# Prompt keys turned by VectorE, the norm factor inside the softmax, and one table load for logarithm and exponential in a hybrid decoder step

## The chip, the cores and the metric

The kernel runs on one core of one Trainium2 chip. The metric is the device time of one execution in microseconds (us). Beside it stands the profiled execution, whose trace gives every instruction of the five engines: TensorE (PE, with its weight loads as PEld), VectorE (DVE), ScalarE (ACT), GpSimd (POOL) and SyncE (SP). POOL and SP issue the DMAs.

## The reference

One layer of a hybrid decoder is computed for 256 prompt tokens and 8 sample sequences of 4 tokens, 288 columns in all, in fp32:

```
xn = rmsnorm(x, norm_mix)
z, xbc, dt, q, k, v, r, g_lr, gate_a, gate_b = split(xn @ w_in)
u = ssd_scan(silu(causal_conv(xbc)), dt, ...) * silu(z)        # Mamba-2 branch, 4 groups
branch_a = rmsnorm_per_group(u, ssd_norm) @ w_ssd_out
glog = log_sigmoid(g_lr @ w_gla_gate + b_gla_gate) / 16
o = gla_scan(q, k, v, glog, ...)                               # gated linear attention, 4 heads
branch_b = (rmsnorm_per_head(o, gla_norm) * silu(r)) @ w_gla_out
h = x + (sigmoid(gate_a) * branch_a + sigmoid(gate_b) * branch_b) @ w_mix_out
# cross-attention, 4 heads of 512, 256 memory tokens; prompt keys and values are
# rmsnorm(mem_prompt) @ w_ck and @ w_cv (also outputs), those of the samples come from a cache
q = rmsnorm(h, norm_cross) @ w_cq
h = h + (softmax(q @ mem_k.T / sqrt(512)) @ mem_v) @ w_co
up = causal_conv(rmsnorm(h, norm_ffn) @ w_up)                  # ConvFFN, 5632 wide
y = rmsnorm(h + (silu(gt) * a) @ w_down, norm_final)
```

The outputs are y, the new states of both branches and of the convolutions, and the prompt's memory keys and values.

## The kernel before, in words

**Projections.** Activations are held transposed: features on the 128 partitions, 288 tokens along the free dimension. `proj` and `proj_w` (L133 to L169) multiply them by a weight matrix, 256 output columns at a time. SyncE loads a weight piece of two row blocks into a tile `raw` (128x512, 256 KB, 6 buffers). `wsplit` (L100) makes two tiles of it, 5 buffers each: ScalarE casts the high part `whi` (L103), VectorE subtracts to get the low part `wlo` (L105). TensorE multiplies three times, high by high and high by low (L148, L149) and low by high (L153). One such step is 12 matmuls of 288 columns; a full projection of 2048 rows and 256 columns has 8 steps and fills two PSUM tiles `acc`, which the consumer function (`cons`) empties. The `acc` tiles have two tags with two buffers each, used in turn, so that a projection takes up the tiles of the one before the last.

**Order of work.** The program stands in a block with a timeline-simulating scheduler (L44). It decides each engine's order of instructions at build time, except where `keep_in_program_order` or a manual schedule holds them. Each engine then executes its list strictly in that order.

**Stages.** First come the memory keys and values of the prompt, written to the outputs o_pmk and o_pmv. Then come eight units, four of the Mamba-2 branch and four of the linear attention (GLA). The scan of each unit is woven with the projections of the next and with the output projection of the one before (`weave`, L180). A unit ends in `finish` (L981): squares are summed over partitions with a matmul by ones (L989), `rstd_from` (L230) takes Ln (L232) and Exp (L233) on ScalarE, and the result is scaled and split into `un`. The group of the Mamba-2 branch also has `gate_early` (L1271), which takes tanh of a quarter of gate_a. A GLA scan begins with `decays` (L1034), with Abs, Exp, Ln (L1045 to L1047) and later Exp (L1053).

Next comes `gate_b` (L1416): the eight projections of the second gate. Its consumer takes tanh of a PSUM tile into `th` (3 buffers, L1418), does two VectorE operations with the branches (L1419, L1420) and splits the result into `mx`. Between these, GpSimd loads four pieces of the merged first branch (`load_mix`, tiles `mar`, 2 buffers), four sample key tiles `kc` of head 0 (`key_load`, 1 MB each), and the residual `hx`. A load that must not come too early is tied to a consumer by a one-column copy on GpSimd from `th` into the tile that is to be loaded. VectorE turns the sample keys in 32x32 blocks (`turn32`, L1386).

`w_mix_out` follows and leaves sums of squares in `sqa`. In cross-attention the next head's query projection (`q_proj`, L1533) is woven with `attend` (L1559) of the present head. The row sum of squares becomes a factor for each of the 288 columns by a matmul with ones (`rstd_of`, L1449), Ln and Exp. The evictions of the queries multiply by that factor (`qs` L1545, `qsm` L1547). `rows_load` brings a head's prompt keys and values in rows; `transpose_half` (L1521) turns the keys with 8 TensorE transposes of 128x128 in a head (L1527) into PSUM, from where they are split into `kTh` and `kTl`. All tiles of keys and values share a ring of five 1 MB buffers (`ring`, L1355). Then come w_co, the ConvFFN (more than a third of the time) and the last norm.

Of the kernel before, what the change touches and what calls it, by code (L numbers as in the profile page):

```python
# [8 lines left out]
F32 = mybir.dt.float32  # L9
F32R = mybir.dt.float32r  # L10
I32 = mybir.dt.int32
ACT = mybir.ActivationFunctionType
# [30 lines left out]
def hybrid_step(ctx: ExitStack, tc: tile.TileContext, I: dict, O: list):  # L43
# [31 lines left out]
    ones = const.tile([P, P], F32, name="ones")  # L75
    V.memset(ones, 1.0)
    epsc = const.tile([P, 3], F32, name="epsc")
    V.memset(epsc[:, 0:1], EPS)
    V.memset(epsc[:, 1:2], 4.0 * EPS)
    fold4 = const.tile([P, NS], F32, name="fold4")  # L80
# [146 lines left out]
    def two(u, n):  # L227
        return lambda k: (u[:, k, :], u[:, n + k, :])

    def rstd_from(pl, ssq, n, four=False):  # L230
        r = pl.tile([P, T], F32, tag="rstd", bufs=1, name="rstd")
        S.activation(r, ssq, ACT.Ln, scale=1.0 / n, bias=epsc[:, 1:2] if four else epsc[:, 0:1])  # L232
        S.activation(r, r, ACT.Exp, scale=-0.5)  # L233
        return r
# [39 lines left out]
    ga_d = dram.tile([P, KT // 2, T], F32, name="ga_d")  # L274
    x_d = dram.tile([D, T], F32, name="x_d")
    h_d = dram.tile([P, KT, T], F32, name="h_d")

    X = halves(bigr, "xn")
    with pool("p0") as p0:
# [736 lines left out]
    def gla_proj(h, out):  # L1016
# [17 lines left out]
        def decays():  # L1034
# [231 lines left out]
            yield from proj(I["w_in"], o + 256 * j2, 256, X, KT, cons)  # L1266

    gq = []
    GH = KT // 4

    def gate_early(t, a):  # L1271

        if t % 2 == 0:
            gq.append(e2("gq"))
        S.activation(gq[-1][:, t % 2, :], a, ACT.Tanh, scale=0.5)
        if t % 2:
            G.dma_start(out=ga_d[:, t - 1:t + 1, :], in_=gq[-1])

# [89 lines left out]
    def rows_load(hd):  # L1368

        t = ktiles[hd, "p"] = ring("kvp")  # L1370
        for w, src in ((0, o_pmk), (1, o_pmv)):
            tc.keep_in_program_order(G.dma_start(out=t[:, 1024 * w:1024 * w + 1024].rearrange("p (m d) -> p m d", m=2),
                                                 in_=src[0, :, hd, :].rearrange("(m p) d -> p m d", p=P)))

    def values(b, hd):
        return I["cache_mem_v"][b, :, hd, :].rearrange("(p h) d -> p h d", h=2)
# [35 lines left out]
        hx.append(m)  # L1412

    load_mix(0)

    def gate_b(t, a):  # L1416
        th = pc.tile([P, T], F32, tag="th", bufs=3, name="th")
        S.activation(th, a, ACT.Tanh, scale=0.5)  # L1418
        V.scalar_tensor_tensor(th, th, 1.0, mb[:, t, :], ALU.add, ALU.mult)  # L1419
        V.tensor_tensor(th, th, mas[t // 4][:, t % 4, :], ALU.add)  # L1420
# [27 lines left out]

    def rstd_of():  # L1449
        ssq = mm_tile()  # L1450
        tc.keep_in_program_order(MM(ssq[:, 0:T], ones, rst.pop(), start=True, stop=True))
        return rstd_from(pb, ssq[:, 0:T], D)

    rst = []
# [33 lines left out]
    for z in (*xqm, pms):  # L1488
        G.memset(z, 0.0)

    def softmax(src, n, out):
        mx = px.tile([P, 1], F32, tag="mx", bufs=3, name="mx")
        V.tensor_reduce(mx[0:n], src, axis=AX.X, op=ALU.max)
        V.tensor_scalar(mx[0:n], mx[0:n], -SC, None, ALU.mult)
        sm = px.tile([P, 1], F32, tag="sm", bufs=3, name="sm")
        S.activation(out, src, ACT.Exp, scale=SC, bias=mx[0:n], accum_out=sm[0:n])
        V.reciprocal(sm[0:n], sm[0:n])
        S.activation(out, out, ACT.Identity, scale=sm[0:n])

    def swapped(t, name):  # L1500

# [5 lines left out]
    def softmax_halves(src, out):  # L1507

        mx = px.tile([P, 1], F32, tag="mx", bufs=3, name="mx")
        V.tensor_reduce(mx, src, axis=AX.X, op=ALU.max)  # L1510
        mo = swapped(mx, "mo")
        V.tensor_scalar(mx, mx, mo, -SC, ALU.max, ALU.mult)
        sm = px.tile([P, 1], F32, tag="sm", bufs=3, name="sm")
        S.activation(out.rearrange("p (m t) -> p t m", t=4), src.rearrange("p (t m) -> p t m", t=4), ACT.Exp, scale=SC, bias=mx,
                     accum_out=sm)
        so = swapped(sm, "so")
        V.tensor_tensor(sm, sm, so, ALU.add)
        V.reciprocal(sm, sm)
        S.activation(out, out, ACT.Identity, scale=sm)

    def transpose_half(kv, d2):  # L1521

        a = mm_tile()
        for d in range(2):
            for m in range(2):
                dd = 2 * d2 + d
                TR(a[:, d * 256 + m * P:d * 256 + (m + 1) * P], kv[:, m, dd * P:(dd + 1) * P], ident)  # L1527
        return a.rearrange("p (d m) -> p d m", m=256)

    qps = []  # L1530
    rc = []

    def q_proj(hd):  # L1533

        if not rc:
            late.append(lambda: mids.append([6, lambda: rc.append(rstd_of())]))
        qp = []
        qps.append(qp)
        for j2 in range(2):
            def cons(j, a, j2=j2):  # L1540
                if j == 0:
                    qp.append((q2("qh"), q2("ql")))
                d = 2 * j2 + j
                qs = px.tile([P, SEQ], F32, tag="qs", bufs=1, name="qs")
# [14 lines left out]
    def attend(hd):  # L1559
# [21 lines left out]
                key_load(hd + 1, c)  # L1581
        yield
        yield
        kvp = ktiles[hd, "p"].rearrange("p (w m d) -> p w m d", w=2, m=2)
        kh, kl = r4("kTh"), r4("kTl")
        for d2 in range(2):
            a = transpose_half(kvp[:, 0], d2)
            split(kh[:, 2 * d2:2 * d2 + 2, :], kl[:, 2 * d2:2 * d2 + 2, :], a)
        yield
        yield  # L1590
        prs = []
        for l in range(2):
# [11 lines left out]
            softmax(a[:, 0:256], P, pp)  # L1604
            prs.append(pp)
            yield
        yield
        vh, vl = v2("vph"), v2("vpl")
        split(vh, vl, kvp[:, 1])
        if more:  # L1610
            key_load(hd + 1, 2)
        yield
# [343 lines left out]
```

## Time and profile before

| | us |
|---|---|
| median of 3 runs (lowest, highest) | 2484.65 (2481.55, 2485.2) |
| the profiled execution | 2484.34 |
| span of its trace, first to last instruction | 2482.6 |
| TensorE busy | 2466.9 |
| VectorE busy | 1769.0 |
| ScalarE busy | 1343.4 |
| GpSimd busy | 436.1 |

The granted TensorE clock was 0.998 over the span. A row of a timeline reads: start in us, duration in us, engine, source line, operation, output tile <- input tiles, shape, count; in brackets the idle time of the engine before it and what ended it. A row of the grouped view reads: busy us, mean ns of one. "The chain of waits" is the chain of work that ended last, each piece with what released it.

### The profile page before, as it was taken

To read this page: it belongs to the slowest core of one execution; us is meant where nothing else is said; L and a number is where in the kernel's file an instruction comes from. 1 tells how busy PE (TensorE), PEld (TensorE's weight loads), DVE (VectorE), ACT (ScalarE), POOL (GpSimd) and SP (SyncE) were. 2 spreads that over 40 slices of the span, in tenths; PEclk is the share of its full clock that TensorE was granted. 3 is DMA by queue.
4 is the path that set the end of the run, shared out by engine and by line. 5 is a ranking of instruction groups with operands and counts; after the bars stand their busy time and mean duration, and the time that the engine had idled before them with its cause. 6 is when DMAs were issued, how large, how long until landed. Compare 5 with 4: busy or idle time off the path is not lost.

```text
span 2482.6 us, 52081 instructions
## 1 busy us (share of the span) xinstructions
PE 2466.9 (99%) x18766; PEld 2387.6 (96%) x18766; DVE 1769.0 (71%) x3794; ACT 1343.4 (54%) x2733; POOL 436.1 (18%) x792
## 2 busy tenths in 40 slices
PE   9999999999999999999999999999999999999998
PEld 8889999999999999999999998999999999999998
DVE  6756778896877666777666577667777676676766
ACT  6656647646464655544555545555555454554545
POOL 3102135143111010110111122402111001020012
PEclk9999999999999999999999999999999999999999
DMA  8877697787769686877777698656555555555555
GB/s 257 250 225 201 167 270 216 205 249 223 230 210 295 200 261 184 249 252 221 234 234 252 204 342 306 195 164 172 170 172 172 172 170 173 170 172 168 170 173 170
DMA packets 457075, 528.66 MB, mean 213 GB/s; under 512 B 40252, under 2 KB 403612, under 8 KB 456784
## 3 DMA queue, kind: packets, MB, share of 16 engines
q1 hardware_dynamic: 420272, 422.39, 56.6%
q0 software_dynamic: 36512, 102.93, 13.0%
q8 instruction: 147, 2.41, 0.4%
q14 instruction: 112, 0.92, 0.1%
q10 hardware_dynamic: 32, 0.01, 0.0%
HBM read 476.41 MB, written 48.76 MB: 212 GB/s over the span
## 4 chain that ended last, share of the span: by engine, by line
PE 95%; DMA 2%; issue 1%; DVE 1%; ACT 0%; POOL 0%; DVEq 0%; POOLq 0%; ACTq 0%
PE acc L149 27%; PE acc L148 27%; PE acc L153 27%; PE acc L328 2%; PE acc L329 2%; PE acc L332 2%; DMA kc<-in_cache_mem_k_dram 1%; PE mm L1239 1%; PE la L1230 1%; PE la L1576 1%; PE mm L1194 0%; DMA raw<-in_w_ssd_out_dram 0%; DMA vc<-in_cache_mem_v_dram 0%; PE la L903 0%; PE mm L924 0%
## 5 line engine op out<-in xcount | busy, mean ns | idle before, releaser
L103 ACT CAST whi<-raw 128x512 fp32r<-128x512 f32 x1464 | 899.7, 618 | 965.2 <-PE acc L149 781.7
L105 DVE TENSOR_TENSOR wlo<-raw,whi 128x512 fp32r<-128x512 f32 x1464 | 996.6, 686 | 549.2 <-ACT whi L103 536.4
L149 PE MATMUL acc<-xn,whi 128*128 128x288 f32 (+1 forms) x1936 | 541.5, 296 | 0.0
L148 PE MATMUL acc<-xn,whi 128*128 128x288 f32 (+1 forms) x1936 | 539.8, 294 | 0.3 <-ACT whi L103 0.3
L153 PE MATMUL acc<-xn,wlo 128*128 128x288 f32 (+1 forms) x1936 | 408.2, 292 | 0.0
L149 PE MATMUL acc<-hf,whi 128*128 128x288 f32 x1408 | 393.1, 296 | 0.0
L148 PE MATMUL acc<-hf,whi 128*128 128x288 f32 x1408 | 388.7, 292 | 0.0
L148 PEld LDWEIGHTS acc<-xn,whi 128*128 128x128 f32 (+1 forms) x1936 | 363.3, 188 | 5.1 <-issue 2.3
L149 PEld LDWEIGHTS acc<-xn,whi 128*128 128x128 f32 (+1 forms) x1936 | 363.7, 188 | 3.6 <-issue 0.4
L153 PEld LDWEIGHTS acc<-xn,wlo 128*128 128x128 f32 (+1 forms) x1936 | 310.4, 188 | 0.9 <-issue 0.4
L153 PE MATMUL acc<-hf,wlo 128*128 128x288 f32 x1408 | 294.5, 290 | 0.0
L149 PEld LDWEIGHTS acc<-hf,whi 128*128 128x128 f32 x1408 | 264.5, 188 | 0.0
L148 PEld LDWEIGHTS acc<-hf,whi 128*128 128x128 f32 x1408 | 264.0, 188 | 0.0
L153 PEld LDWEIGHTS acc<-hf,wlo 128*128 128x128 f32 x1408 | 226.3, 188 | 0.1
L149 PE MATMUL acc<-pr,whi 128*128 128x288 f32 x704 | 196.6, 295 | 0.0
L148 PE MATMUL acc<-pr,whi 128*128 128x288 f32 x704 | 194.8, 293 | 0.0
L1749 POOL COPY fsp<-fst 128x16 f32<-128x16 f32 x88 | 37.3, 427 | 650.7 <-DVE av L1761 431.4
L153 PE MATMUL acc<-pr,wlo 128*128 128x288 f32 x704 | 147.3, 290 | 0.0
L148 PE MATMUL acc<-un,whi 128*128 128x288 f32 x512 | 143.0, 295 | 2.5 <-ACT vT L1020 1.5
L149 PE MATMUL acc<-un,whi 128*128 128x288 f32 x512 | 142.9, 295 | 0.0
L149 PEld LDWEIGHTS acc<-pr,whi 128*128 128x128 f32 x704 | 132.3, 188 | 0.0
L148 PEld LDWEIGHTS acc<-pr,whi 128*128 128x128 f32 x704 | 132.0, 188 | 0.0
(551 smaller groups left out, 4301.9 us busy)
## 6 DMA issues: line engine op xcount, KB each, us to landing
raw<-in_w_in_dram SPq DMA_DIRECT2D x480, 256.0 KB
raw<-in_w_up_dram SPq DMA_DIRECT2D x352, 256.0 KB
raw<-in_w_down_dram SPq DMA_DIRECT2D x176, 256.0 KB
raw<-in_w_ck_dram SPq DMA_DIRECT2D x64, 256.0 KB
raw<-in_w_cv_dram SPq DMA_DIRECT2D x64, 256.0 KB
raw<-in_w_ssd_out_dram SPq DMA_DIRECT2D x64, 256.0 KB
sin<-in_state_gla_dram POOLq DMA_DIRECT2D x32, 512.0 KB, 6.2
out_dram<-sin SPq DMA_DIRECT2D x32, 512.0 KB
```

What stands on the lines that cost most here:

```text
L103: S.copy(hi, raw)
L105: V.tensor_tensor(lo, raw, hi, ALU.subtract)
L148: MM(a, hi[:, k, cs], xh, start=(k0 + s0 + k == 0), stop=False)
L149: MM(a, hi[:, k, cs], xl, start=False, stop=False)
L153: MM(a, lo[:, k, cs], xh, start=False, stop=(k0 + s0 + k == nk - 1))
L328: MM(accs[m], mn_hi[:, kk, ms_], hi[:, 0, :], start=(kk == 0), stop=False)
L329: MM(accs[m], mn_lo[:, kk, ms_], hi[:, 0, :], start=False, stop=False)
L332: MM(accs[m], mn_hi[:, kk, ms_], lo[:, 0, :], start=False, stop=(kk == KT - 1))
L1230: MM(osa[NS * j:NS * j + NS, :], qdm[:, k, b, :], sins[b][:, k, :], start=False, stop=(q == 1 and k == 0))
L1239: MM(a, kb[:, k * P:(k + 1) * P], vst, start=True, stop=True)
L1576: MM(ssc[NS * c:NS * c + NS, 0:P], xq[:, j, u, :], kt[:, j], start=(j == 0), stop=(j == 15))
L1749: G.tensor_copy(sp[:, :, 0:2], st.rearrange("p (b k) -> p b k", k=2))
```

## The change

Three things change at once.

**Tables.** A new function `lnexp` loads the ScalarE table set that holds both logarithm and exponential (`natural_log_exp_and_others`). It is called in `finish` of units 0 to 6 ahead of Ln, in `decays` ahead of its Exp and Ln, and in `rstd_of`. A one-column copy on ScalarE (tile `junk1`) can tie the load to a tile that must be there first. In units 0 and 2 the load waits for the next pair of `gate_early` tanh operations, in the others for the low part of the sum of squares.

**Prompt keys.** 64 GpSimd DMAs (`prompt_key_load`) issued ahead of gate_b bring the prompt keys of all four heads in 32-row blocks of 128-byte runs (32 KB each, 2 MB in all) into two ring tiles `kp`. Eight VectorE block transposes (`prompt_key_turn`, through `turn32`) within gate_b's consumers t = 2 to 9 turn them, and four stores put them into a DRAM tile `kT_d`. `rows_load` reads that, and `transpose_half` is gone: the split reads SBUF instead of PSUM.

**Norm factor.** `row_scales` computes the norm's factor for each query row (128x3) with three matmuls of one column, Ln, Exp and two small scalings. It is used as scale and in the bias of the softmax exponentials. The query evictions no longer multiply: `qs` goes, and ScalarE copies `qsm`.

```diff
+    def lnexp(after=None):
+        if after is not None:
+            S.copy(junk1, after)
+        tc.keep_in_program_order(S.preload_act_table_set(LNEXP))
...
+            if len(fin) in (0, 2):
+                after = len(gq)
+                while len(gq) == after or len(tanhs) % 2:
+                    yield
+                lnexp(gq[-1][:, 1, 0:1])
+            else:
+                lnexp(sp[1][:, 0:1])
...
             S.activation(ke, qe, ACT.Abs)
+            lnexp()
             S.activation(ke, ke, ACT.Exp, scale=-1.0)
...
     def rows_load(hd):
         t = ktiles[hd, "p"] = ring("kvp")
-        for w, src in ((0, o_pmk), (1, o_pmv)):
-            tc.keep_in_program_order(G.dma_start(out=t[:, 1024 * w:1024 * w + 1024]..., in_=src...))
+        tc.keep_in_program_order(G.dma_start(out=t[:, 0:1024], in_=kT_d[hd]))
+        tc.keep_in_program_order(G.dma_start(out=t[:, 1024:2048]..., in_=o_pmv...))
+    def prompt_key_load(n):
+        t = ring("kp")
+        kps.append(t)
+        for i in range(2):
+            v = t[:, 1024 * i:1024 * i + 1024].rearrange("p (b f j) -> p f b j", b=8, j=32)
+            rows = o_pmk[0, :, 2 * n + i, :].rearrange("(b t) (f q j) -> q f t b j", t=32, q=4, j=32)
+            for q in range(4):
+                for f in range(4):
+                    tc.keep_in_program_order(G.dma_start(out=v[32 * q:32 * q + 32, f], in_=rows[q, f]))
+    def prompt_key_turn(c):
+        if c < 8:
+            turn32(kps[c // 4], c % 4)
+        if c % 2 == 0 and c:
+            n, i = divmod(c // 2 - 1, 2)
+            tc.keep_in_program_order(G.dma_start(out=kT_d[2 * n + i], in_=kps[n][:, 1024 * i:1024 * i + 1024]))
...
     load_mix(0)
+    for n in range(2):
+        prompt_key_load(n)
...
     (in gate_b)
+        if 2 <= t < 11:
+            prompt_key_turn(t - 2)
...
     (in softmax and softmax_halves)
-        S.activation(out, src, ACT.Exp, scale=SC, bias=mx[0:n], accum_out=sm[0:n])
+        S.activation(out, src, ACT.Exp, scale=rc[0][:, l:l + 1], bias=mx, accum_out=sm)
...
-    def transpose_half(kv, d2):
+    def row_scales():
+        sq = rst.pop()
+        sqs_ = px.tile([P, 2, 2, 2, 16], F32, name="sqs")
+        for th in range(2):
+            G.tensor_copy(sqs_[:, th], sq[:, SEQ:T]...)
+        a = mm_tile()
+        for i in range(3):
+            w = sq[:, i * P:(i + 1) * P] if i < 2 else sqs_.rearrange("p h u r l -> p (h u r l)")
+            tc.keep_in_program_order(MM(a[:, i:i + 1], w, ones[:, 0:1], start=(i == 0), stop=(i == 2)))
+        rs = px.tile([P, 6], F32, name="rs")
+        S.activation(rs[:, 0:3], a[:, 0:3], ACT.Ln, scale=1.0 / D, bias=epsc[:, 0:1])
+        S.activation(rs[:, 0:3], rs[:, 0:3], ACT.Exp, scale=-0.5)
+        V.tensor_scalar(rs[:, 3:6], rs[:, 0:3], -SC, None, ALU.mult)
+        V.tensor_scalar(rs[:, 0:3], rs[:, 0:3], SC, None, ALU.mult)
+        return rs
...
     (in q_proj)
-                V.tensor_tensor(qs, a[:, 0:SEQ], rc[0][:, 0:SEQ], ALU.mult)
-                split(qp[j2][0][:, j, :], qp[j2][1][:, j, :], qs)
-                V.tensor_tensor(qsm[:, d], a[:, SEQ:T], rc[0][:, SEQ:T], ALU.mult)
+                split(qp[j2][0][:, j, :], qp[j2][1][:, j, :], a[:, 0:SEQ])
+                S.copy(qsm[:, d], a[:, SEQ:T])
...
     (in attend)
-            a = transpose_half(kvp[:, 0], d2)
-            split(kh[:, 2 * d2:2 * d2 + 2, :], kl[:, 2 * d2:2 * d2 + 2, :], a)
+            split(*(x[:, ds_, :].rearrange("p f (b j) -> p f b j", j=32) for x in (kh, kl)),
+                  kvp[:, 0:1024].rearrange("p (b f j) -> p f b j", b=8, j=32)[:, ds_])
```

The scheduler orders the engines anew. Three places show how; the lines of the kernel after stand some lines further down than those of before (L103 becomes L104, L232 L239, L1418 L1459).

The first place is ScalarE's list at the norm of unit 2 (third group of the Mamba-2 branch), before:

```order
L103 CAST whi<-raw 128x512
L1275 ACTIVATE gq<-acc 128x288
L103 CAST whi<-raw 128x512
L232 ACT_TABLE_LOAD
L232 ACTIVATE rstd<-mm,epsc 128x288
L832 ACTIVATE m<-ab,tokc 128x128 x4
L233 ACT_TABLE_LOAD
L233 ACTIVATE rstd<-rstd 128x288
```

The same place after:

```order
L1292 ACTIVATE gq<-acc 128x288
L234 COPY junk_78<-gq 128x1
L235 ACT_TABLE_LOAD
L104 CAST whi<-raw 128x512
L239 ACTIVATE rstd<-mm,epsc 128x288
L840 ACTIVATE m<-ab,tokc 128x128 x4
L104 CAST whi<-raw 128x512
L240 ACTIVATE rstd<-rstd 128x288
```

One of two table loads is gone, and the other has moved ahead of a weight cast, right behind the second tanh of the pair (gq). A load of the tanh set comes later, with the next convolution's tanh.

The second place is ScalarE's list in gate_b, where the third and fourth pair of gate tiles is taken out of PSUM (th<-acc is the tanh, mx<-th the split's cast), before:

```order
L1418 ACTIVATE th<-acc 128x288
L103 CAST whi<-raw 128x512
L1418 ACTIVATE th<-acc 128x288
L197 ACTIVATE mx_15704<-th 128x288
L103 CAST whi<-raw 128x512
L197 ACTIVATE mx_15704<-th 128x288
L103 CAST whi<-raw 128x512 x6
L1418 ACTIVATE th<-acc 128x288
L103 CAST whi<-raw 128x512
L1418 ACTIVATE th<-acc 128x288
```

The same place after, beginning with the tanh of t = 3:

```order
L1459 ACTIVATE th<-acc 128x288
L104 CAST whi<-raw 128x512
L198 ACTIVATE mx_15724<-th 128x288
L104 CAST whi<-raw 128x512 x14
L1459 ACTIVATE th<-acc 128x288 x3
L198 ACTIVATE mx_15724<-th 128x288 x3
L1459 ACTIVATE th<-acc 128x288
```

Between the tanh of t = 3 and that of t = 4 there now stand 15 weight casts, where before a pair of tanh came every eight casts; the tanh of t = 4, 5 and 6 stand in a row.

The third place is VectorE's list at the same point of gate_b (there the tiles t = 6 and 7 before, 4 to 7 after):

Before:

```order
L1386 STREAM_TRANSPOSE kc<-kc 128x512 x4
L105 TENSOR_TENSOR wlo<-raw,whi 128x512 x2
L1419 SCALAR_TENSOR_TENSOR th<-th,mb 128x288
L105 TENSOR_TENSOR wlo<-raw,whi 128x512
L1419 SCALAR_TENSOR_TENSOR th<-th,mb 128x288
L1420 TENSOR_TENSOR th<-th,mar 128x288 x2
```

The same point after:

```order
L106 TENSOR_TENSOR wlo<-raw,whi 128x512 x8
L1425 STREAM_TRANSPOSE kp<-kp 128x512 x2
L1460 SCALAR_TENSOR_TENSOR th<-th,mb 128x288
L1425 STREAM_TRANSPOSE kp<-kp 128x512
L1460 SCALAR_TENSOR_TENSOR th<-th,mb 128x288
L1425 STREAM_TRANSPOSE kp<-kp 128x512
L1460 SCALAR_TENSOR_TENSOR th<-th,mb 128x288
L1461 TENSOR_TENSOR th<-th,mar 128x288 x3
L199 SCALAR_TENSOR_TENSOR mx_15724<-th,mx_15724 128x288 x3
L1460 SCALAR_TENSOR_TENSOR th<-th,mb 128x288
L1461 TENSOR_TENSOR th<-th,mar 128x288
L106 TENSOR_TENSOR wlo<-raw,whi 128x512
```

Fifteen operations other than wlo now stand in a row there; before, at most four transposes of kc stood between two wlo.

On GpSimd the 64 loads of kp stand between the load of the first mar piece and the copy that ties the second to the gate's first tile; before, that copy came right behind.

More of the change, by code (lines that the diff above doesn't have):

```diff
@@ L77, in hybrid_step @@
     epsc = const.tile([P, 3], F32, name="epsc")
+    junk1 = const.tile([P, 1], F32, name="junk1")
     V.memset(epsc[:, 0:1], EPS)
@@ L276, in hybrid_step @@
     h_d = dram.tile([P, KT, T], F32, name="h_d")
+    kT_d = dram.tile([4, P, 1024], F32, name="kT_d")
     X = halves(bigr, "xn")
@@ L1450, in rstd_of @@
         ssq = mm_tile()
-        tc.keep_in_program_order(MM(ssq[:, 0:T], ones, rst.pop(), start=True, stop=True))
+        a = rst.pop()
+        lnexp(a[:, 0:1])
+        tc.keep_in_program_order(MM(ssq[:, 0:T], ones, a, start=True, stop=True))
         return rstd_from(pb, ssq[:, 0:T], D)
@@ L1511, in softmax_halves @@
         mo = swapped(mx, "mo")
[L1512 removed]
+        V.tensor_scalar(mx, mx, mo, rc[0][:, 5:6], ALU.max, ALU.mult)
         sm = px.tile([P, 1], F32, tag="sm", bufs=3, name="sm")
[L1514 removed]
+        S.activation(out.rearrange("p (m t) -> p t m", t=4), src.rearrange("p (t m) -> p t m", t=4), ACT.Exp, scale=rc[0][:, 2:3], bias=mx,
                      accum_out=sm)
@@ L1519, in softmax_halves @@
         S.activation(out, out, ACT.Identity, scale=sm)
-    def transpose_half(kv, d2):
[L1523 to L1528, printed above, removed]
     qps = []
     rc = []
+    def row_scales():
+        sq = rst.pop()
+        sqs_ = px.tile([P, 2, 2, 2, 16], F32, name="sqs")
+        for th in range(2):
+            G.tensor_copy(sqs_[:, th], sq[:, SEQ:T].rearrange("p (u l) -> p u l", u=2).unsqueeze(2).to_broadcast([P, 2, 2, 16]))
+        a = mm_tile()
[8 more added lines that the diff above has]
+        return rs
     def q_proj(hd):
         if not rc:
-            late.append(lambda: mids.append([6, lambda: rc.append(rstd_of())]))
+            late.append(lambda: mids.append([6, lambda: rc.append(row_scales())]))
         qp = []
```

25 lines of the change are left out of this document (14 added, 11 removed).

## The prediction, on record before the changed kernel ran

> **What bounds the kernel now.** I read the page's busy times first, then TensorE's view of waits, then the timelines around each wait. The busy row shows an engine that hardly ever rests:
>
> ```profile
> PE 2466.9 (99%) x18766; PEld 2387.6 (96%) x18766; DVE 1769.0 (71%) x3794; ACT 1343.4 (54%) x2733; POOL 436.1 (18%) x792
> ```
>
> The span is 2482.6 us, so all of TensorE's idle time is 2482.6 - 2466.9 = 15.7 us. A change can do three things here: take TensorE work out, take some of the 15.7 us away, or add waits. Work of the other engines counts only where TensorE waits for it. The waits view names those places:
>
> ```profile
> PE acc L148 <- ACT vT L1020: 1.5, 2, 1.1
> PE la L1576 <- DVE xqm L1555: 1.3, 3, 0.5
> PE mm L365 <- DVE epsc L78: 1.1, 1, 1.1
> PE acc L148 <- DVE ma L1010: 1.0, 1, 1.0
> PE mm L771 <- ACT rstd L232: 0.8, 1, 0.8
> ```
>
> The line mm L365 is the kernel's start, which the change leaves alone. The first, the fourth and the fifth lie in the Mamba-2 units, the second in cross-attention. Together these four are 4.6 us.
>
> **Transposes out, row scales in.** Both are TensorE work on the path, and the chain of waits has their prices; the third row is the grouped view of an operation of the same form as the new one (weights of 128 columns, one column of ones):
>
> ```profile
> 1387.05 0.48 PE mm L1451 x2
> 1412.75 0.87 PE mm L1527 x8
> ```
> ```profile
> L1896 PE MATMUL acc<-ones,sq 128*128 128x1 f32 x12 | 1.5, 243 | 0.0
> ```
>
> Eight transposes of a head take 0.87 us on the path, four heads 4 x 0.87 = 3.48 us. TensorE is busy right behind them, so all of it can come off: -3.48. The three matmuls of `row_scales` are six records (an fp32 matmul leaves two), half of the 12 records that are busy for 1.5 us: at most 0.75 us, in place of 0.48. That is +0.27 at most, since records overlap; I take +0.2. The GpSimd copies that feed them can run as soon as the sums of squares are there; GpSimd, busy for 18% of the span, has room for them.
>
> **Tables.** The wait for rstd at L771 is in unit 1:
>
> ```profile
> 488.22 1.28 ACT L232 ACT_TABLE_LOAD   x1
> 489.51 0.50 ACT L232 ACTIVATE rstd<-mm,epsc 128x288 f32<-128x288 f32 x1
> 490.46 1.28 ACT L233 ACT_TABLE_LOAD   x1
> ```
> ```profile
> 490.07 0.65 PE L771 MATMUL mm<-ident,xsT 128*128 128x128 f32 x4 [0.83 <-ACT rstd L232]
> ```
>
> The chain through that wait is the first load, 1.28 us, and the 0.50 us of Ln. In the new order of unit 1 the load stands behind the same weight casts as before, with a small copy ahead of it. So the load doesn't start earlier and this wait stays, perhaps 0.2 us longer; only the second load goes, behind the wait. In unit 2 the position does change:
>
> ```profile
> 586.87 0.40 ACT L1275 ACTIVATE gq<-acc 128x288 f32<-128x288 f32 x1
> 587.92 0.62 ACT L103 CAST whi<-raw 128x512 fp32r<-128x512 f32 x1 [0.65 <-ACT gq L1275]
> 588.56 1.28 ACT L232 ACT_TABLE_LOAD   x1
> 589.85 0.50 ACT L232 ACTIVATE rstd<-mm,epsc 128x288 f32<-128x288 f32 x1
> 591.54 1.28 ACT L233 ACT_TABLE_LOAD   x1
> ```
>
> The load now begins at 586.87 + 0.40 = 587.27, half in ScalarE's idle 0.65 us. From 593 us on ScalarE is ahead by the second load and that idle time, 1.28 + 0.65 = 1.9 us. Until 606 us it runs without a break, and what comes late behind it are weight tiles:
>
> ```profile
> 601.74 0.40 PE L148 MATMUL acc<-xn,whi 128*128 128x288 f32 x1 [0.31 <-ACT whi L103]
> 619.74 0.40 PE L148 MATMUL acc<-un,whi 128*128 128x288 f32 x1 [0.35 <-ACT vT L1020]
> 621.92 0.40 PE L148 MATMUL acc<-un,whi 128*128 128x288 f32 x1 [1.12 <-ACT vT L1020]
> 635.52 0.37 PE L148 MATMUL acc<-un,whi 128*128 128x288 f32 x1 [0.98 <-DVE ma L1010]
> ```
>
> The first three add up to 1.78 us and fit a lead of 1.9 us; the fourth has VectorE as its releaser and needn't move. With all four the gain is 2.76 us, about 3.2 with 0.1 us of restart for each. With none it is 0, and unit 1 may cost 0.3. I take 1.78 for the first three less 0.3: -1.5, between -3.2 and +0.3. The added reload of the tanh set costs ScalarE 1.28 us a unit (the length of a load above) beside TensorE's work: ScalarE is busy for 54%, and the reload stands ahead of a convolution's tanh, which no wait above names. The tables ahead of the GLA decays and the FFN norm count as nothing for the same reason; if that cover were gone, one such load would cost up to 1.28 us.
>
> [...]
>
> **The key loads and gate_b.** The 64 loads are issued by GpSimd ahead of gate_b, where it was idle:
>
> ```profile
> 1156.11 0.54 POOL L1404 DMA_DIRECT2D mar<-mg_d  x1
> 1190.68 0.58 POOL L1403 COPY mar<-th 128x1 f32<-128x1 f32 x1 [34.03 <-DVE th L1420]
> ```
> ```profile
> 318.44 3.23 POOL L753 DMA_DIRECT2D sqr<-in_state_ssd_dram  x5
> 331.38 0.22 POOL L640 COPY cv<-scst 128x27 f32<-128x27 f32 x1
> ```
>
> The nearest load in form is sqr (32 partitions, 128-byte runs, twice the size). Five take 3.23 us, 0.65 each; all 16 of a set are issued from 318.44 to 331.38, 0.81 each with their waits. So 64 loads last 42 to 52 us and end between 1198 and 1208. The copy for mar waits until then, 8 to 18 us later than before. It brings the gate's second quarter, first used for t = 4, behind 1227 us: nobody waits for it. The extra traffic (2 MB in, 2 MB out, and 2 MB less read from the output) runs beside weight loads and costs nothing so long as these don't fall behind.
>
> The order does cost something. In the new list ScalarE takes the tanh of t = 4 only behind the 15th weight cast after that of t = 3. That tanh frees the PSUM tile that the fifth projection needs:
>
> ```profile
> 1226.72 0.41 ACT L1418 ACTIVATE th<-acc 128x288 f32<-128x288 f32 x1 [0.48 <-PE acc L153]
> 1227.48 0.62 ACT L103 CAST whi<-raw 128x512 fp32r<-128x512 f32 x1 [0.34 <-PE acc L153]
> 1228.01 0.40 ACT L1418 ACTIVATE th<-acc 128x288 f32<-128x288 f32 x1
> ```
> ```profile
> 1227.24 0.29 PE L148 MATMUL acc<-xn,whi 128*128 128x288 f32 x1
> ```
>
> The cast at 1227.48 is that 15th one; before, it stands between the tanh of t = 6 and of t = 7, which are the rows around it. It is bound by TensorE's progress, so tanh t = 4 can begin at 1228.01 and ends at 1228.4. The fifth projection begins at 1227.24 today, so TensorE waits 1.2 us. VectorE then does 15 operations without a wlo, four of them turns:
>
> ```profile
> 1223.20 0.69 DVE L105 TENSOR_TENSOR wlo<-raw,whi 128x512 fp32r<-128x512 f32 x1 [0.87 <-ACT whi L103]
> 1226.15 2.49 DVE L1386 STREAM_TRANSPOSE kc<-kc 128x512 f32<-128x512 f32 x4 [2.26 <-DMA kc<-in_cache_mem_k_dram]
> ```
> ```profile
> L1419 DVE SCALAR_TENSOR_TENSOR th<-th,mb 128x288 f32<-128x288 f32 x16 | 7.2, 453 | 0.7 <-ACT th L1418 0.6
> 1177.32:1227.24 49.92, 49.92 (x386) 49.92 (x385) 30.91 (x56) 24.80 (x45) 6.14 (x8) 1.00 0.77 231
> ```
>
> Four turns are 2.49 us and 11 operations of 0.45 are 5.0 at most, as much as 7.4 us. The longest break between two wlo of before, from 1223.89 to 1228.6, is 4.7 us with no TensorE wait (busy 49.92 of 49.92 us). The lead lasts for at least that, so the excess is between 0 and 2.7 us; I take 0.8, since the PSUM wait shifts TensorE back while VectorE catches up. Gate_b then costs 1.2 + 0.8 = +2.0, between 0 and +4.
>
> **Attention.** VectorE is relieved of the multiplication qs, four times in a head, and TensorE arrives 0.87 us earlier in each head. What it meets there is a transfer:
>
> ```profile
> 1493.79 3.05 PE L1576 MATMUL la<-kc,xqm 128*32 128x128 f32 x104 [0.40 <-DVE xqm L1555]
> ```
> ```profile
> DVE kc L1386 <- DMA kc<-in_cache_mem_k_dram: 6.2, 2, 3.3
> ```
> ```profile
> 1460.00:1500.00 40.00, 38.86 (x401) 35.01 (x400) 29.81 (x76) 19.19 (x47) 8.61 (x13) 1.00 0.93 335
> ```
>
> VectorE waited 6.2 us for kc transfers between 1460 and 1500 us, with the DMAs 93% busy over that stretch. VectorE's saving can remove up to the 1.3 us of waits; an earlier TensorE can meet the same transfer with up to 1.7 us more wait (two heads' transposes). These are of like size: 0, between -1.3 and +1.7.
>
> **The sum.** -3.48 + 0.2 - 1.5 + 2.0 + 0 = -2.8. The profiled execution took 2484.34, 0.3 below the median of 2484.65; 2484.34 - 2.8 gives 2481.5. A measurement of this kernel can tell about 0.2%, 5 us, from no change; the borders are 2479.7 and 2489.6.
>
> **The rivals.**
> 1. Everything is gained (0.24): ScalarE's lead removes all four waits (-3.2), VectorE's saving those of attention (-1.3), and gate_b absorbs its bunch. The sum is -3.48 + 0.2 - 3.2 - 1.3 = -7.8, 2476.5. For it speaks how short each wait is, against it the PSUM tile that stands behind a fixed order.
> 2. Attention gives back (0.13): the transfers set the pace there, and half of the transposes turns into waits for kc. -2.8 + 1.7 = -1.1, 2483.2. The busy DMAs speak for it; that TensorE waited for only 1.3 us there speaks against.
> 3. The GpSimd queue is late, and the kernel slower (0.13). Behind the 64 loads stand three copies (0.58 each), then the load of mar for t = 4:
>
> ```profile
> mar<-mg_d POOLq DMA_DIRECT2D x4, 576.0 KB, 5.3
> ```
>
> It must be issued by about 1224 to be there at 1230, so the 64 loads may last (1222 - 1156.7) / 64 = 1.02 us each. At 1.2 us they end at 1233.5, and with 1.7 of copies, 0.5 of issue and 5.3 to land mar is there at 1241, 11 us late. VectorE stands at the addition of t = 4 with all wlo queued behind it, and TensorE starves: -3.48 + 0.2 - 1.5 + 11 = +6.2, 2490.5. The measured 0.65 and 0.81 us speak against it, the narrowness of the gap, 64 against 16 in a row, speaks for it. [...]
>
> My forecast has the other 0.50, with a range of its own of 2479 to 2485. Faster by over 0.2% is rival 1 and the low end of the forecast, 0.24 + 0.08 = 0.32. Slower is rival 3 and a gate_b at its worst, 0.13 + 0.02 = 0.15. Within is the rest, 0.53. The range of 2476 to 2487 leaves out the lower half of rival 1 (below 2476, some 0.1) and most of rival 3 (some 0.1).
>
> **What would show it.** TensorE's busy time should fall by about 3.3 us. In unit 2 the table load should stand right behind the tanh of gq and the first three waits between 601 and 622 should be gone; at L771 in unit 1 a wait of 0.8 to 1.0 should remain. In gate_b the 64 loads should end by 1208, and TensorE should wait for the tanh of t = 4 for about 1.2 us at the fifth projection. I would be wrong if the loads last beyond 1222, if TensorE waits for kc or xqm in attention for over 3 us, or if gate_b shows no wait at all.

## The result: slower by 0.7%, and where the profile after shows it

The changed kernel takes 2501.32 us (median of 6 runs, 2498.34 to 2502.92) against 2483.78 us before on the same chip. The ratio is 1.0068, with a 95% interval of 1.0058 to 1.0079. I had forecast 2481.5.

TensorE's busy time went up, though 32 transposes are gone. This is the busy row of the page after:

```profile
PE 2475.3 (99%) x18738; PEld 2394.4 (96%) x18738; DVE 1770.8 (71%) x3772; ACT 1338.4 (54%) x2752; POOL 475.5 (19%) x862
```

The waits view of TensorE after has a new first line: weights that come late. Before, whi was waited for once, 0.3 us.

```profile
PE acc L149 <- ACT whi L104: 8.7, 6, 3.1
PE acc L149 <- DVE ma L1025: 3.8, 2, 3.3
PE mm L779 <- ACT rstd L239: 1.0, 1, 1.0
PE mm L932 <- ACT cst L633: 0.8, 1, 0.8
PE acc L149 <- ACT th L1459: 0.8, 1, 0.8
```

Three marks tell the stages apart: the ones matmul of the last unit's norm, the matmuls of the norm factor ahead of attention, and the ones matmul ahead of the ConvFFN. Of each line I use the first or the last start. Before:

```profile
L992 PE MATMUL mm<-sqa,ones x2: 405/406/406, 1143.8 to 1144.0; 128*128 128x288 f32 x2
L1451 PE MATMUL mm<-sqa,ones x4: 405/406/406, 1386.9 to 1654.2; 128*128 128x288 f32 x4
```

After:

```profile
L1007 PE MATMUL mm<-sqa,ones x2: 403/404/405, 1163.1 to 1163.4; 128*128 128x288 f32 x2
L1578 PE MATMUL mm<-ones,sqa x4: 166/250/250, 1411.2 to 1411.4; 128*128 128x1 f32 x4
L1496 PE MATMUL mm<-sqa,ones x2: 403/404/404, 1672.5 to 1672.7; 128*128 128x288 f32 x2
```

At the end of the units the changed kernel is 1163.1 - 1143.8 = 19.3 us late. After gate_b and w_mix_out it is 1411.2 - 1386.9 = 24.3 late, and after attention 1672.7 - 1654.2 = 18.5. The end is 2501.0 - 2482.6 = 18.4 late. So the units lose 19.3, gate_b and w_mix_out lose 5.0, attention gains 5.8, and the ConvFFN does nothing. I had expected -1.5, +2.0 and -3.3.

The loss in the units begins around 320 us, ahead of the first norm: there no table load, key or norm factor of the change has yet been executed. What differs there is what the DMAs achieve. The view by windows (the last two columns are the DMA share and GB/s), before and then after:

```profile
320.00:340.00 20.00, 20.00 (x153) 19.84 (x153) 16.33 (x39) 8.40 (x15) 8.98 (x15) 1.00 1.08 324
420.00:440.00 20.00, 20.00 (x153) 19.84 (x152) 12.41 (x30) 9.39 (x20) 11.29 (x19) 1.00 1.05 291
540.00:560.00 20.00, 20.00 (x149) 19.64 (x148) 18.89 (x49) 8.58 (x15) 6.27 (x10) 1.00 1.08 315
```
```profile
320.00:340.00 20.00, 19.21 (x143) 18.59 (x142) 11.12 (x27) 5.59 (x10) 11.66 (x19) 1.00 1.10 256
420.00:440.00 20.00, 20.00 (x152) 19.83 (x151) 12.29 (x25) 9.31 (x20) 13.64 (x22) 1.00 1.09 247
540.00:560.00 20.00, 19.00 (x139) 18.25 (x139) 16.66 (x44) 4.88 (x9) 13.68 (x21) 1.00 1.09 236
```

In both kernels the DMA engines are full there (a share of 1.05 to 1.10), but they move 324, 291 and 315 GB/s before and 256, 247 and 236 after. These are stretches in which weights and the states of a scan arrive together: from 320 to 340 us, 13 loads of raw and 14 of sqr are issued before, 7 and 16 after. ScalarE's waits for weights from 300 to 760 us show the same, before and then after:

```profile
ACT whi L103 <- DMA raw<-in_w_in_dram: 20.0, 18, 2.5
```
```profile
ACT whi L104 <- DMA raw<-in_w_in_dram: 52.1, 35, 5.6
```

A wait of 3.07 us costs more than itself here. This is TensorE's timeline behind it, and the windows around it, whose column ahead of the DMA share is the granted clock:

```profile
569.60 0.60 PE L149 MATMUL acc<-xn,whi 128*128 128x288 f32 x1 [3.07 <-ACT whi L104]
570.00 0.44 PE L150 MATMUL acc<-xn,whi 128*128 128x288 f32 x1
570.24 0.44 PE L149 MATMUL acc<-xn,whi 128*128 128x288 f32 x1
```
```profile
568.00:570.00 2.00, 0.41 (x2) 0.41 (x2) 1.12 (x2) 1.60 (x3) 0.00 (x0) 0.81 1.06 317
570.00:572.00 2.00, 2.00 (x9) 2.00 (x9) 1.46 (x3) 0.88 (x2) 0.71 (x1) 0.50 1.06 315
```

At clock 0.50 a matmul starts every 0.24 us, where it is every 0.13 at 1.00. TensorE counts as busy meanwhile (2.00 of 2.00 us): part of its higher busy time is this. It is seen behind three waits of the units, of 2.57, 3.07 and 3.28 us (they end at 446, 569 and 653 us).

### The profile page after: what moved, and what is told of

It reads as the page before. It is cut to its first block, busy times and chain, and to the rows that moved or that the text cites. A ratio compares the mean times of both kernels' runs of the same rounds, so it can differ in the third digit from the quotient of the medians.

```text
span 2501.0 us, 52130 instructions
## 1 busy us (share of the span) xinstructions
PE 2475.3 (99%) x18738; PEld 2394.4 (96%) x18738; DVE 1770.8 (71%) x3772; ACT 1338.4 (54%) x2752; POOL 475.5 (19%) x862
## 4 chain that ended last, share of the span: by engine, by line
PE 96%; DMA 3%; DVE 1%; ACT 0%; issue 0%; DVEq 0%; SPq 0%; ACTq 0%
PE acc L150 27%; PE acc L149 27%; PE acc L154 27%; PE acc L336 2%; DMA raw<-in_w_in_dram 2%; PE acc L340 2%; PE acc L337 2%; PE mm L1255 1%; PE la L1246 1%; PE la L1627 1%; PE la L1685 1%; PE mm L1210 0%; DMA raw<-in_w_ssd_out_dram 0%; PE la L911 0%; ACT whi L104 0%; PE mm L1225 0%
## 5 line engine op out<-in xcount | busy, mean ns | idle before, releaser
L104 ACT CAST whi<-raw 128x512 fp32r<-128x512 f32 x1464 | 902.2, 618 | 1004.1 <-PE acc L150 776.1
L154 PE MATMUL acc<-xn,wlo 128*128 128x288 f32 (+1 forms) x1936 | 410.7, 295 | 0.0
L154 PEld LDWEIGHTS acc<-xn,wlo 128*128 128x128 f32 (+1 forms) x1936 | 310.5, 188 | 2.3 <-issue 1.0
L154 PE MATMUL acc<-hf,wlo 128*128 128x288 f32 x1408 | 294.7, 290 | 0.0
L154 PEld LDWEIGHTS acc<-hf,wlo 128*128 128x128 f32 x1408 | 226.3, 188 | 0.1
L154 PE MATMUL acc<-pr,wlo 128*128 128x288 f32 x704 | 147.4, 290 | 0.0
```

What stands on the lines that cost most here:

```text
L104: S.copy(hi, raw)
L154: MM(a, lo[:, k, cs], xh, start=False, stop=(k0 + s0 + k == nk - 1))
```

## Experiments on the address

**Theory.** The change adds a constant, junk1, a column of 4 bytes, which takes 32 bytes of each partition. In the built program every SBUF tile behind it lies 32 bytes higher: the first weight tile at byte 18720 instead of 18688 = 73 x 256. The address theory says that this shift, not the new order or the new work, costs the time. The rival, the order theory, says that the table loads' new places reorder the units.

**e1_pad** shifts the tiles of the kernel before, with no other change:

```diff
-    epsc = const.tile([P, 3], F32, name="epsc")
+    epsc = const.tile([P, 9], F32, name="epsc")
```

> The kernel before with one constant tile (epsc) widened from 3 to 9 columns, so that every SBUF tile behind it lies 32 bytes higher, as in the changed kernel; all instructions and their order are those of before. Address theory (the changed kernel's weights and states come late because the DMAs write to tiles that begin 32 bytes off): 12 to 20 us slower than before, 2496 to 2504 us, with waits of TensorE for whi between 320 and 660 us and lower GB/s at a DMA share above 1. Order theory (the table loads' new places reorder the units and make the weights late): as before, 2483.8 within 3 us.

Measured: 2509.66 us, ratio 1.0100 (1.0086 to 1.0114), 25.5 us slower than before with not one instruction moved, some 5 us beyond the address theory's range. Its ScalarE waits for weights (300 to 760 us), and TensorE's waits for them, are like those of the changed kernel:

```profile
ACT whi L103 <- DMA raw<-in_w_in_dram: 56.2, 36, 5.0
```
```profile
PE acc L148 <- ACT whi L103: 8.5, 5, 4.4
PE acc L148 <- ACT vT L1020: 2.6, 1, 2.6
```

**e2_aligned** keeps the changed kernel's order and takes the shift away:

```diff
-    dtb = const.tile([32, 1], F32, name="dtb")
-    alog = const.tile([32, 1], F32, name="alog")
+    dtal = const.tile([32, 2], F32, name="dtal")
+    dtb, alog = dtal[:, 0:1], dtal[:, 1:2]
```

> The changed kernel with two 32-byte constants (dtb, alog) put into one tile, so that the tiles behind lie where they lie in the kernel before; the order of all instructions is that of the changed kernel. Address theory: 15 to 20 us faster than the changed kernel, 2479 to 2486 us; the waits for whi in the units mostly gone. Order theory: as the changed kernel, 2501 within 3 us.

Measured: 2482.50 us, ratio 0.9993 (0.9984 to 1.0002). The 18.8 us are gone, and with them the waits for raw (the same view as above) and the late weights in the units:

```profile
ACT whi L104 <- DMA raw<-in_w_in_dram: 22.9, 19, 2.9
```
```profile
PE acc L149 <- DVE ma L1025: 2.6, 1, 2.6
PE mm L779 <- ACT rstd L239: 1.0, 1, 1.0
PE acc L149 <- ACT th L1459: 0.8, 1, 0.8
PE acc L149 <- ACT whi L104: 0.7, 2, 0.4
```

The order theory falls: with the order of the change and the addresses of before, the kernel is as fast as before; with the order of before and the addresses of the change, it is slow.

**e3_shift64** shifts the changed kernel by 64 bytes (`junk1` as the first column of a tile of 16), **e4_shift128** the kernel before by 128 (`epsc` with 40 columns), **e6_shift160** the kernel before by 160 (`epsc` with 48).

> The changed kernel with junk1 widened to 64 bytes, so that all tiles behind lie 64 bytes higher than before (a multiple of 64, not of 128); order as in the changed kernel. Address theory with a 64-byte border: as the aligned one, 2479 to 2486 us. Address theory with a border of 128 bytes or more: as the changed kernel, 2496 to 2504 us. Order theory: 2501 within 3 us.

> The kernel before with all SBUF tiles behind the constants 128 bytes higher (epsc widened to 40 columns); weight tiles then begin at a multiple of 128, not of 256. Border of 128 bytes: as before, 2484 within 3 us. Border of 256 bytes or more: slow as with 32 bytes, 2495 us or more.

> The kernel before with all SBUF tiles behind the constants 160 bytes higher (128 + 32), order as before. If what counts is the tiles' place within 128 bytes: slow as with 32 bytes, 2500 to 2512 us. If what counts is a chance of this one placement (some tiles that happen to collide): anything, most likely within 5 us of 2484 or of the 2490 of 128 bytes.

Measured: 2499.92 us for 64 bytes in the changed order, 17.4 above the aligned one; 2489.74 us, ratio 1.0031 (1.0018 to 1.0043), for 128, outside both of its ranges; 2504.95 us, ratio 1.0079 (1.0065 to 1.0092), for 160. The two shifts that leave 32 over a multiple of 128 are both slow, so it isn't one unlucky placement; a shift by 128 costs 5 us, a fifth of the 25, but more than nothing: the border isn't 128 alone.

**Which tiles?** **e5_late32** moves only the tiles of the start and of the eight units that lie behind `acs`, by 32 bytes; **e5_early32** moves these by 128 and all other tiles behind `epsc`, weights and activations among them, by 32. In the built program the tiles of gate_b, attention and the ConvFFN move with the weights, and not with those of the scans as the two expectations say:

```diff
-    acs = p1.tile([P, 8], F32, name="acs")
+    acs = p1.tile([P, 16], F32, name="acs")[:, 0:8]
```
```diff
-    epsc = const.tile([P, 3], F32, name="epsc")
+    epsc = const.tile([P, 16], F32, name="epsc")
...
-    acs = p1.tile([P, 8], F32, name="acs")
+    acs = p1.tile([P, 32], F32, name="acs")[:, 0:8]
```

> The kernel before with the weight tiles where they are, and only the tiles of the scans and stages behind them (state loads sqr and sin) 32 bytes higher. If the state loads are what suffers: 2495 to 2510 us. If the weight loads are: as before, 2484 within 4 us.

> The kernel before with the weight tiles (raw, whi, wlo) and the activations 32 bytes higher, but the tiles of the scans (state loads sqr and sin, and all behind them) 128 bytes higher. If the weight loads into raw are what suffers: as with everything 32 bytes higher, 2500 to 2510 us. If the state loads are: as before, 2484 within 4 us.

Measured: 2507.11 us, ratio 1.0092 (1.0078 to 1.0105), and 2504.17 us, ratio 1.0078 (1.0064 to 1.0092). Each half alone costs some 20 us, so the times don't name the tiles. The traces say more. TensorE's busy rows, of the early and then of the late shift:

```profile
PE 2484.4 (99%) x18766; PEld 2399.4 (96%) x18766; DVE 1770.7 (71%) x3794; ACT 1343.3 (54%) x2733; POOL 435.8 (17%) x792
```
```profile
PE 2485.0 (99%) x18766; PEld 2400.4 (96%) x18766; DVE 1769.7 (71%) x3794; ACT 1342.1 (54%) x2733; POOL 435.1 (17%) x792
```

Most of the loss is now TensorE taking longer over the same work, 17.5 and 18.1 us more than 2466.9. Much of it sits where the edits move the two operands of a product apart: the weights lie 32 bytes off the units' tiles modulo 128 in both runs, and not in e1_pad or in the change. The projection of the memory shows it without a wait, here its products of wlo, before, in e1_pad, early and late:

```profile
L332 PE MATMUL acc<-wlo,mn_hi 128*128 128x512 f32 x256 | 79.0, 391 | 0.0
L332 PE MATMUL acc<-wlo,mn_hi 128*128 128x512 f32 x256 | 79.1, 391 | 0.0
L332 PE MATMUL acc<-wlo,mn_hi 128*128 128x512 f32 x256 | 80.8, 397 | 0.0
L332 PE MATMUL acc<-wlo,mn_hi 128*128 128x512 f32 x256 | 80.4, 397 | 0.0
```

The three groups of this projection take 5.2 and 4.3 us more than before (0.4 in e1_pad), the three with `un` 7.2 and 7.6 (1.7 in e1_pad); in the changed kernel it is 0.2 and 2.6 us. Over the span the granted clock was 0.996 and 0.997, where it was 0.998 before, so some of the extra time can be that of a lower clock. Still a large part of the 17.5 and 18.1 us is a loss that the change doesn't have. The late weights, which it has, are in one half alone. ScalarE's waits for them from 300 to 760 us, early and then late:

```profile
ACT whi L103 <- DMA raw<-in_w_in_dram: 20.4, 22, 3.0
```
```profile
ACT whi L103 <- DMA raw<-in_w_in_dram: 49.2, 30, 5.9
```

With the weight tiles 32 bytes higher the waits are those of before (20.0 us); with the units' tiles 32 bytes higher they come near those of e1_pad (56.2).

**The last three** ask whether the DMAs' writes or the engines' own accesses suffer. The pads stand in the weights' pool, with a memset on GpSimd; x0_base128 has 128 bytes between raw and whi, x1_raw32 has 32 ahead of raw (`epsc` with 16 columns) and 96 behind, x2_eng32 has 32 between raw and whi and 96 behind wlo:

```diff
     def wsplit(raw):
+        if not pads:
+            pads.append(wp.tile([P, 32], F32, tag="pad", bufs=1, name="pad"))
+            G.memset(pads[0], 0.0)
         hi = wp.tile(list(raw.shape), F32R, tag="whi", bufs=WB, name="whi")
```

> Base for the two next: the kernel before with an unused pad of 128 bytes between the DMA's weight tiles (raw, where they were) and all tiles behind (whi, wlo, activations, states), which lie 128 bytes higher; one memset of the pad is added on GpSimd. All theories: like the shift of all tiles by 128 bytes or better, 2484 to 2490 us.

> As the base, but the weight tiles raw, which the DMAs write, lie 32 bytes higher; all that TensorE reads lies as in the base. If the DMAs' writes into tiles that begin off 128 bytes are slow: 2495 to 2505 us. If the engines' accesses to such tiles are: as the base within 3 us.

> As the base, but the split weights whi and wlo, which only engines write and read, lie 32 bytes off a multiple of 128 and raw where it was. If the DMAs' writes are slow: as the base within 3 us. If the engines' accesses are: 2495 to 2505 us.

Measured: 2488.08 us, ratio 1.0015 (1.0005 to 1.0025); 2491.10 us, ratio 1.0029 (1.0018 to 1.0040); 2530.76 us, ratio 1.0195 (1.0179 to 1.0210). The theory that the weight loads' writes into shifted tiles are slow falls: raw alone costs 3 us over its base, and the two intervals overlap. The shift of whi and wlo against everything else costs 43 us over the base, the most of all runs and far above the 2495 to 2505 expected, and without more waits: TensorE is idle for 2529.6 - 2514.0 = 15.6 us, as before (15.7). Its products of wlo take 297 to 299 ns in every projection with 288 columns, where they take 290 to 294 in x0_base128. The projection of the memory is as slow as in the two halves:

```profile
L340 PE MATMUL acc<-wlo,mn_hi 128*128 128x512 f32 x256 | 80.7, 397 | 0.0
```

One window of the ConvFFN, before and in x2_eng32 (the count behind the second number is TensorE's matmuls):

```profile
1900.00:2000.00 100.00, 100.00 (x771) 100.00 (x770) 67.34 (x148) 48.14 (x97) 12.37 (x24) 1.00 0.56 171
```
```profile
1900.00:2000.00 100.00, 100.00 (x752) 100.00 (x751) 70.44 (x162) 49.23 (x105) 13.24 (x26) 1.00 0.54 166
```

At a granted clock of 1.00 it does 752 matmuls in the time of 771, 2.5% fewer. In e1_pad, where weights and activations are shifted alike, the ConvFFN kept its pace (771 in the same window). So the runs show at least two effects. TensorE was slower where its weights lay 32 bytes off its other operand modulo 128: with all activations in x2_eng32 (the 297 to 299 ns above), with the tiles of the start and the units in e5_early32 and e5_late32 (397 ns against 391 for wlo with mn_hi, 300 against 293 for wlo with `un`). And where the tiles of the start and the units lay 32 bytes higher, the DMAs delivered less in the units and the weights came late: 247, 247 and 256 GB/s from 320 to 340 us in e5_late32, e1_pad and the changed kernel, against 324 before, with 49.2, 56.2 and 52.1 us of ScalarE's waits against 20.0. In e5_early32, where these tiles lie 128 bytes higher, it was 272 GB/s, with waits of 20.4. The first is not what hit the change, which moves weights and activations alike (wlo with mn_hi takes 391 ns in it). The second is, and its inner cause stays open: which of the units' tiles count, and whether it is the transfers into them or the engines' accesses, was not tried.

In all, other start addresses of its tiles made the kernel before up to 47 us slower, of 2484 (x2_eng32, with two memsets more on GpSimd).

## Experiments on the parts

**p_tables**: the table part alone, aligned (`lnexp`, its three places, and `dtal` as above).

> The kernel before with the table part alone (lnexp in the norms and decays), tiles aligned as before. Address theory and my prediction's term: 1 to 3 us faster than before, 2481 to 2483 us. Order theory: 10 to 18 us slower, 2494 to 2502 us, since the reordering comes from this part.

Measured: 2483.28 us, ratio 1.0001 (0.9992 to 1.0010). That excludes the 10 to 18 us of the order theory. A gain isn't shown, but the interval, -2.0 to +2.5 us, has room for the 1.5 us forecast.

**p_norm**: `row_scales`, the softmax and the evictions of the change, with `transpose_half` kept.

> The norm factor in the softmax alone, aligned as before: VectorE loses four multiplications a head, TensorE keeps its transposes. If the attention gain beyond the transposes comes from VectorE's relief: 1.5 to 3 us faster than before, about 2482, with less wait at L1576. If it comes from the turned keys: within 1 us of before.

Measured: 2487.10 us, ratio 1.0007 (0.9999 to 1.0016). The relief of VectorE alone gives nothing that shows. In the trace the three waits for xqm (1.3 us before) are gone, but one wait of 1.66 us stands at the same product, and the view names no releaser for it; attention takes 1657.7 - 1388.1 = 269.6 us, 2.3 more than before.

**p_keysnorm**: keys and norm factor, without the tables. **v_spread_keys**: the same, with 16 of the 64 key loads ahead of gate_b and the rest behind its tiles; each is loaded by a call for a quarter:

```diff
     load_mix(0)
-    for n in range(2):
-        prompt_key_load(n)
+    prompt_key_load(0, 0)
...
+        if t == 2:
+            prompt_key_load(0, 1)
+        if t == 4:
+            prompt_key_load(1, 0)
+        if t == 6:
+            prompt_key_load(1, 1)
-        if 2 <= t < 11:
-            prompt_key_turn(t - 2)
+        if 5 <= t < 14:
+            prompt_key_turn(t - 5)
```

> Prompt keys and norm factor as in the change, without the table part, aligned as before; gate_b keeps the bunch of tanh and turns. If the bunch costs what the traces show (2.5 to 3 us): 2 to 3 us slower than the version with spread keys, 2482 to 2484 us, with a wait of TensorE for the tanh of t = 4 and for whi behind it. If the bunch is free: as that version, 2481.

> Prompt keys and norm factor without the table part, aligned as before, and three quarters of the 64 key loads moved behind gate_b's tiles t = 2, 4 and 6, the turns to t = 5 to 12, so that ScalarE's list in gate_b has the tanh in pairs behind every eight weight casts as before. My theory (the bunch in gate_b costs about 3 us, the attention part gains 5.8): 2477 to 2480 us, no wait of TensorE in gate_b. Rival (the key loads' transfers, not the order, delay gate_b): waits stay there, 2480 to 2483 us.

Measured: 2484.03 us, ratio 0.9997 (0.9988 to 1.0006), with the bunch; 2481.20 us, ratio 0.9986 (0.9977 to 0.9995), spread. The second time lies in the rival's range, but the rival's waits aren't there. The bunch is at work as the order had it, here in TensorE's timeline of p_keysnorm; in the version with spread keys gate_b has no wait at all:

```profile
1228.03 0.40 PE L148 MATMUL acc<-xn,whi 128*128 128x288 f32 x1 [0.76 <-ACT th L1442]
1237.97 0.79 PE L153 MATMUL acc<-xn,wlo 128*128 128x288 f32 x4 [0.73 <-DVE wlo L105]
1247.55 0.40 PE L148 MATMUL acc<-xn,whi 128*128 128x288 f32 x1 [0.96 <-ACT whi L103]
```

**v_all_spread**: the whole change, aligned (`dtal`), with the spread keys.

> The whole change, tiles aligned as before, with the key loads spread over gate_b. If the table part is worth nothing, as it measured alone: as the version without it, 2481 within 1.5 us. If it adds my 1.5 us once the rest is in order: 2479.5.

Measured: 2478.96 us (2478.22 to 2481.25, 11 runs), ratio 0.9980 (0.9971 to 0.9989): faster than both kernels, and 0.5 us from the 2479.5 that I expected if the tables are worth 1.5. All that TensorE still waits for but the start:

```profile
PE acc L149 <- DVE ma L1025: 1.0, 1, 1.0
PE mm L779 <- ACT rstd L239: 1.0, 1, 1.0
PE acc L149 <- ACT whi L104: 0.7, 1, 0.7
```

## Why the prediction was wrong, point by point

**The failed step** stands in the part on tables: "with a small copy ahead of it". I gave the copy a price of 0.2 us and the tile that it writes none. The prediction took for granted that work that no edit touches keeps its time. The tile's 32 bytes moved everything behind it, and that cost 18.8 us, more than all terms together. No rival named it. With it taken away (e2_aligned), 2482.5 us were measured and 2481.5 forecast. So the other terms are compared with that kernel, whose marks are:

```profile
L1007 PE MATMUL mm<-sqa,ones x2: 405/406/406, 1144.4 to 1144.7; 128*128 128x288 f32 x2
L1578 PE MATMUL mm<-ones,sqa x4: 167/250/250, 1390.2 to 1390.5; 128*128 128x1 f32 x4
L1496 PE MATMUL mm<-sqa,ones x2: 405/406/406, 1651.6 to 1651.9; 128*128 128x288 f32 x2
```

Units +0.6, gate_b and w_mix_out 3.3 - 0.6 = +2.7, attention -2.3 - 3.3 = -5.6. Each is a difference of two executions, and such differences scatter. The edit of p_tables has nothing in gate_b and w_mix_out and only a table load in attention; with its marks at 1143.3, 1388.4 and 1653.5 us it takes 2.0 us more than before in the one and 2.2 less in the other.

**Tables: right in mechanism, size open.** Forecast -1.5, measured +0.6 in this execution. The load in unit 2 stands right behind the tanh pair, as the order had it, the three waits between 601 and 622 us are gone, and at L771 (now L779) 1.0 us remains, within my 0.8 to 1.0. But the fourth wait, which I let stand at 0.98, became 2.64 here, which takes 1.66 of the 1.78 us back. The load behind the tanh:

```profile
589.26 0.19 ACT L234 COPY junk<-gq 128x1 f32<-128x1 f32 x1
589.47 1.28 ACT L235 ACT_TABLE_LOAD   x1
```

In v_all_spread that wait is 1.0 again, and the units are 0.4 us ahead of before, by the mark at their end:

```profile
L1007 PE MATMUL mm<-sqa,ones x2: 405/406/406, 1143.4 to 1143.6; 128*128 128x288 f32 x2
```

The mark scatters by as much as the term: it lies at 1143.3 to 1144.4 us in the three aligned executions with the table part and at 1143.6 to 1145.0 in the four without. By the ratios to before, the table part is worth nothing alone (1.0001), 1.0 us beside the bunched keys (0.9993 against 0.9997) and 1.5 us beside the spread ones (0.9980 against 0.9986). The intervals overlap, so the runs don't tell nothing from the forecast.

**gate_b: right in mechanism.** Forecast +2.0, measured +2.7, of which the waits are 1.1. TensorE waits for the tanh of t = 4 at the fifth projection, 0.76 us where I had 1.2, and once for a weight behind the bunch:

```profile
1228.85 0.40 PE L149 MATMUL acc<-xn,whi 128*128 128x288 f32 x1 [0.76 <-ACT th L1459]
1248.45 0.40 PE L149 MATMUL acc<-xn,whi 128*128 128x288 f32 x1 [0.33 <-ACT whi L104]
```

With 0.1 us of restart for each that is 1.3 us: the first product behind the wait starts at 1228.85 and the next at 1229.09, 0.24 us later, where it is 0.13 without a wait. The remaining 1.4 are no waits. The two versions with spread keys have the same 1.4 (244.5 us against 243.1) without any wait, and p_tables, without any key load, has 2.0; so they needn't come from the change at all. The 64 loads end as forecast, 0.57 to 0.58 us each, in GpSimd's timeline of e2_aligned:

```profile
1161.35 5.21 POOL L1404 DMA_DIRECT2D kp<-out_dram  x9 [4.01 <-PE acc L154]
1191.65 8.04 POOL L1404 DMA_DIRECT2D kp<-out_dram  x14 [0.37 <-DMA kp<-out_dram]
```

They start at 1161.4, 4.7 us later than I put them, since the first waits until a product of TensorE (L154) has ended, and end at 1199.7, inside my 1198 to 1208. The rival of a late GpSimd queue is refuted: 0.60 us a load in all, where 1.02 was its point; the 1.2 us that its sum takes was an assumption, which no run shows.

**Attention: at least what I forecast.** Forecast -3.3 with the row scales, measured -5.6 against before and -3.4 against p_tables (1653.5 - 1388.4 = 265.1 us against 261.7). All waits there are gone, 1.5 us of before that I had set at 0 (with a bound of -1.3). The rival that attention gives the transposes back is refuted. That VectorE's relief brings the rest was my reason, and p_norm doesn't support it: without the turned keys the relief gave nothing. Whether the two parts are needed together or the keys alone do it stays open; keys alone were not tried.

**The sum.** -3.48 + 0.2 - 1.5 + 2.0 = -2.8 was, in the aligned kernel, -2.3 of span, and by the medians -1.7 with an interval that takes in zero. Rival 1, with everything gained (-7.8), wasn't reached even by v_all_spread, -5.1 of span.

## What to carry to other kernels

A new tile is an edit to every address behind it: compare the addresses of the tiles before and after, and keep the size of the constants' region as it was, before any term of the change is costed. When a stage is slower that the change doesn't touch, shift the old kernel by the same bytes; if it gets as slow, the rest of the change hasn't been measured yet. And a list of transfers ahead of a loop can make the scheduler bunch other engines' work behind them (here with 2.45 us of waits in gate_b of p_keysnorm); spread over the loop, the same transfers left no wait there. Where a shift of addresses is tried on a part of the tiles, list what it moves against what: two operands moved apart brought a loss of their own here, 43 us in x2_eng32 over its base.

## What the runs showed of the hardware that I had not expected

- Start addresses of SBUF tiles changed the time at equal instructions: +25.5 us for 32 bytes, +20.6 for 160, +5.1 for 128 (kernel before); +17.4 for 64 (changed order). With full DMA engines (a share of 1.08 and 1.10 from 320 to 340 us) the delivered rate fell from 324 GB/s before to 256 in the changed kernel.
- With whi and wlo 32 bytes off, TensorE did 752 matmuls where it did 771, at a granted clock of 1.00. With the tiles of the start and the units off instead (e5_early32, e5_late32), a product of wlo with mn_hi took 397 ns where it took 391.
- Behind waits of 2.57, 3.07 and 3.28 us in the changed kernel the granted clock was 0.50 for about 3 us. Behind one of 2.64 us in e2_aligned it was 1.00 (636 to 642 us). The runs show no length of wait that divides the two.
